# Other pairs, other shares: a change to the order and the engines of a Strassen weight gradient

## The chip, the cores and the metric

The kernel runs on one core of a Trainium2 chip. The metric is the device time of one execution in microseconds; the time before is 169.47 us, the median of three runs from 169.40 to 169.53. An instruction stands in one of five in-order queues: TensorE (PE, products), VectorE (DVE), ScalarE (ACT), GpSimd (POOL, which issues the loads here) and SyncE (SP, which issues the output).

## The reference

```python
def setup_inputs():
    batch, m, k, n = 16, 512, 1024, 768
    ...

def reference(input, grad_output):
    return np.einsum('bmk,bmn->kn', input, grad_output).astype(np.float32)
```

All 16 x 512 = 8192 rows are summed over: the output is X^T G, 1024 x 768, for X of 8192 x 1024 and G of 8192 x 768.

## The kernel before

**Slices and units.** The 8192 rows are 64 slices of 128 rows. Two slices make a unit; `LOADS` (line 11) has one letter for each of 32 units. An "s" unit is two plain items, one slice each. A "P" unit is one item, a Strassen pair. GpSimd loads every slice with two DMAs that turn float32 into bfloat16: G at line 100, X at line 102. Only slice 0 and slice 1's X come another way, as float32 over the queues of SyncE and ScalarE (lines 74 to 77), and are rounded by VectorE and ScalarE (`round_by`, line 191). The buffers of the loads are rings of 14 units (`PAIRS_HELD`); those of the sums of pairs are rings of 9 (`SUMS_HELD`). TensorE, VectorE and ScalarE keep the order in which the code records their instructions; for GpSimd's loads the order is made when the program is built.

**Quarters and products.** The output is cut into quarters A, B, C, D (A and B the upper 512 rows of k, A and C the left 384 columns). Each quarter takes four PSUM banks, one for each block q of 128 rows. A plain item gives A, B, C and D a product for each q: 16 matmuls of 128 x 128 by 128 x 384. A pair needs 28 matmuls instead of 32: 7 products m, n, o, p, q, A, D, four blocks each. For them VectorE makes six sums a pair (`sum_g1` to `sum_x3`, lines 114 to 143: g1 and g2 write `ge`, x1 and x2 write `xe`, g3 and x3 overwrite half of `gp` and `xp`). The products A and D go straight into the quarters; m to q are gathered in `macc` and added to the quarters at the end, in 24 "shares" (`top1` to `low3`, lines 154 to 174).

**Visits.** `ORDER` (line 14) writes the order of the work out by hand. "A6" means: bring stream A up to its item 6. A step with "!" closes the visit: its four banks are evicted into `acc` or `macc` (`shut`, line 275). Between opening and closing a visit holds half of PSUM (one of two `slots`), so two visits are open at once. The numbers are fills: the one ahead of the letter, and the four behind the "!", ahead of the eviction of each bank, say how many sums or shares VectorE does there; they are taken from one list, `filler` (line 176), sums first, pair by pair, then shares block by block (line 181).

**Evictions.** A bank is evicted either by VectorE, which adds it to the sum in SBUF (line 284; a copy, line 282, when the sum is new), or by ScalarE[...]: it copies the old sum into the bank before the visit (the "seed", line 256) and the bank back afterwards (line 280). `CARRIED` gives ScalarE blocks 2 and 3 of every visit but the last ones of the quarters.

**Start and end.** After ten wide and two narrow warm-up matmuls, the first products are A and C of slice 0; the right half of slice 0's G is rounded when step 2 is reached (line 335), on VectorE behind the evictions of C1. At the end the finished quarters leave in pieces of 192 KB (line 288); the last block of D is computed as 256 and 128 columns, so that its first part leaves sooner (lines 312 to 325).

Of the kernel before, what the change touches and what calls it, by code (L numbers as in the profile page):

```python
# [7 lines left out]

P = 128

LOADS = "sssPssssPsPsPPPPPPPPPPPPPPPsssss"


ORDER = (
    "A1 C1!0,0,0,0 D1 D2!0,0,0,0 A2 B1 B2 B3!0,0,0,0 A3 C4!0,0,0,0 A4 A5 B4 B5 B6!0,0,0,0 A6 "
    "C6!0,0,0,0 D6 6A7 D8!0,0,0,0 A8 o1!0,0,0,0 A9 B8!0,0,0,0 A10 C9 C10!0,0,0,0 A11 "
    "q1!0,0,0,0 A12 D12 A13 D13 A14!0,0,0,0 D14!0,0,0,0 n1 C14!0,0,0,0 B13 B14 6n2!0,0,0,0 "
    "B15 p1 p2!0,0,0,0 B16!0,0,0,0 m1 m2 A17!0,0,1,1 D18 4m3!0,0,0,0 D19 D20 B18!0,0,0,0 "
    "C18!0,0,1,1 A21 D21 4A22!0,0,0,0 D22 o4!2,0,1,1 q4 2D23!3,0,0,0 q5 n5 3n6!0,0,0,0 q6 p5 "
    "p6!6,0,0,0 q7 o7!1,0,0,2 m7 3q8!1,0,0,0 m8 A25 A26!5,0,0,0 m9 p9!1,0,0,2 D27 "  # L20
    "3m10!1,0,0,0 D28 n10!3,0,0,2 D29 A29!2,0,1,1 o11 2o12!2,0,0,0 D30 q12 4D31!1,0,0,0 q13 "
    "p12 p13!5,0,0,0 q14 m14!2,1,0,1 n14!2,0,0,2 q15 o15 4q16!0,0,0,0 o16 D34!2,0,1,1 "
    "A34!1,1,0,3 o17 n17 3o18!0,0,0,0 n18!0,0,0,0 A35 m18!0,0,0,0 A39 q18!0,0,0,0 p18!0,0,0,0 "
    "A41 A43 C22 C24 C26 A46!13,0,0,0 B23 B24 B28!6,0,0,0 C28!5,0,0,0 D46!0,0,0,0 "
).split()

WARMUP = [512] * 10 + [128] * 2
PAIRS_HELD = 14
SUMS_HELD = 9

CARRIED = (2, 3)
COPIED = CARRIED or (1, 3)


@with_exitstack
def kernel(
# [6 lines left out]
    nc = tc.nc  # L43
# [4 lines left out]
    _, _, N = grad_output.shape  # L48
    S = B * M // P
    KH = K // 2  # L50
    NH = N // 2
    Q = KH // P

    X = input.rearrange("b m k -> (b m) k")
    G = grad_output.rearrange("b m n -> (b m) n")
# [17 lines left out]
    gf = pairs.tile([P, N], f32, name="gf", tag="gp")  # L73
# [18 lines left out]
    xg = []  # L92
    for u, kind in enumerate(LOADS):
        pool = pairs if u else head
        xp = pool.tile([P, 2, K], bf16, name="xp", tag="xp")
        gp = pool.tile([P, 2, N], bf16, name="gp", tag="gp")
        for h in range(2):
            s = 2 * u + h
            if s > 0:
                nc.gpsimd.dma_start(out=gp[:, h, :], in_=G[s * P : (s + 1) * P, :])  # L100
            if s > 1:
                nc.gpsimd.dma_start(out=xp[:, h, :], in_=X[s * P : (s + 1) * P, :])  # L102
            if kind == "s":
                items.append(("s", xp[:, h, :], gp[:, h, :]))
        if kind == "P":
            items.append(("P", xp, gp))
        xg.append((xp, gp))
# [68 lines left out]
    filler = []  # L176
    for i, item in enumerate(items):
        if item[0] == "P":
            filler += [(f, i) for f in (sum_g1, sum_g2, sum_g3, sum_x1, sum_x2, sum_x3)]
    if filler:  # L180
        filler += [(f, q) for q in range(Q) for f in (top1, top2, top3)]
        filler += [(f, q) for q in range(Q) for f in (low1, low2, low3)]
    filler.reverse()

    def fill(n):
        for _ in range(n):
            f, i = filler.pop()
            f(i)


    def round_by(engine, dst, src, c0, c1):
        copy = nc.vector.tensor_copy if engine == "DVE" else nc.scalar.copy
        copy(out=dst[:, c0:c1], in_=src[:, c0:c1])  # L193

    x0, x1, g0 = items[0][1], items[1][1], items[0][2]
# [34 lines left out]
    def sum_of(p, q):  # L230
        if p in SLOT:
            return macc[:, SLOT[p], q, :]
        row = q if p in "AB" else Q + q
        return acc[:, row, 0:NH] if p in "AC" else acc[:, row, NH:N]

    done = {p: 0 for p in streams}
    fresh = {p: True for p in streams}
    slots = [0, 1]
    used = set()

    def visit(p, upto, close, ahead, last):
        items_now = streams[p][done[p] : upto]
        done[p] = upto
        opening = p not in opened
        if opening:

            tail = p in "ABCD" and streams[p][upto - len(items_now)] > LAST_PAIR - 2
            slot = slots.pop(0)
            banks = []
            for q in range(Q):  # L250
                name = f"bank{slot * Q + q}"
                bank = psum.tile([P, 512], f32, name=name)[:, 0:NH]
                carried = q in CARRIED and not fresh[p] and not tail
                if carried:
                    assert name in used
                    nc.scalar.copy(out=bank, in_=sum_of(p, q))  # L256
                used.add(name)
                banks.append((bank, carried))
            opened[p] = (slot, banks)
        slot, banks = opened[p]  # L260
        final = upto == len(streams[p])

        def mm(q, j):
            stat, mov = operands(p, items_now[j], q)
            bank, carried = banks[q]
            nc.tensor.matmul(  # L266
                bank,
                stat,
                mov,
                start=opening and j == 0 and not carried,  # L270
                stop=close and j == len(items_now) - 1,
                skip_group_check=carried,
            )

        def shut(q):
            fill(ahead[q])
            bank, carried = banks[q]
            dst = sum_of(p, q)
            if carried or (fresh[p] and q in COPIED):
                nc.scalar.copy(out=dst, in_=bank)  # L280
            elif fresh[p]:
                nc.vector.tensor_copy(out=dst, in_=bank)  # L282
            else:
                nc.vector.tensor_add(out=dst, in0=bank, in1=dst)  # L284
            if final and p in "ABCD":
                row = q if p in "AB" else Q + q
                c0 = 0 if p in "AC" else NH
                nc.sync.dma_start(out=OUT[:, row, c0 : c0 + NH], in_=dst)

        if len(items_now) == 1:  # L290
            for q in range(Q):
                mm(q, 0)
            if close:
                for q in range(Q):
                    shut(q)
        else:
            for q in range(Q):
                if last and q == Q - 1 and opening:
                    break
                for j in range(len(items_now)):  # L300
                    mm(q, j)
                if close:
                    shut(q)
            else:
                q = None
            if q is not None:

                fill(ahead[q])
                dst = sum_of(p, q)
                row = q if p in "AB" else Q + q  # L310
                b0 = 0 if p in "AC" else NH
                for c0, c1, name in ((0, 256, None), (256, NH, f"bank{slots[0] * Q}")):
                    bank = banks[q][0] if name is None else psum.tile([P, 512], f32, name=name)
                    for j in range(len(items_now)):
                        stat, mov = operands(p, items_now[j], q)
                        nc.tensor.matmul(  # L316
                            bank[:, 0 : c1 - c0],
                            stat,
                            mov[:, c0:c1],
                            start=j == 0,  # L320
                            stop=j == len(items_now) - 1,
                        )
                    d = dst[:, c0:c1]
                    nc.vector.tensor_add(out=d, in0=bank[:, 0 : c1 - c0], in1=d)  # L324
                    nc.sync.dma_start(out=OUT[:, row, b0 + c0 : b0 + c1], in_=d)
        if close:
            fresh[p] = False
            del opened[p]
            slots.append(slot)

    for n, step in enumerate(ORDER):
        step, _, ahead = step.partition("!")
        at = next(c for c in step if c.isalpha())
        before, upto = step.split(at)
        if n == 2:
            round_by("DVE", g0, gf, NH, N)
            round_by("DVE", x1, xf[1], 4 * P, 6 * P)
            round_by("ACT", x1, xf[1], 6 * P, 8 * P)
            round_by("DVE", x1, xf[1], 0, 2 * P)
            round_by("ACT", x1, xf[1], 2 * P, 4 * P)  # L340
        fill(int(before or 0))
        ahead = [int(a) for a in ahead.split(",")] if ahead else None
        visit(at, int(upto), ahead is not None, ahead, n == len(ORDER) - 1)
    assert not filler and not opened


# [28 lines left out]
```

## Time and profile before

| what | value |
|---|---|
| median of 3 runs | 169.47 us |
| the profiled execution, its span | 169.8 us, 168.0 us |
| matmuls: whole ones of 384 columns, parts of the last block, warm-up | 940, 24, 12 |
| ScalarE: evictions, seeds | 92 of 483 ns, 74 of 495 ns |
| VectorE: evictions that add, that copy | 89 of 553 ns, 18 of 553 ns |
| VectorE: long shares, short shares | 16 of 954 ns, 8 of 558 ns |
| sums of a pair: g1, g2, g3, x1, x2, x3 | 553, 353, 553, 687, 421, 688 ns |
| loads by GpSimd | 125, 8.5 us from issue to landing |
| output pieces | 17, about 2.0 us from issue to landing |

A row of the timeline gives start and length in us, the engine, the line, the operation and its tiles, how many followed each other, and in brackets how long the engine had been idle and what ended it. The slices are fortieths of the span, 4.2 us each; a digit is a tenth of busy time. [...]the starts in the timeline tell what one instruction keeps the engine from the next.

### The profile page before, as it was taken

The page shows a single profiled execution, that of the slowest core. Times are in us where ns is not written, and L with a number is a line of the kernel's source. Part 1 is how long each engine was busy: PE and PEld are TensorE (multiplying, and loading weights), DVE is VectorE, ACT ScalarE, POOL GpSimd, SP SyncE. Part 2 cuts the span into 40 slices and gives each one's busy share as a digit, 9 for nine tenths or more (in the row PEclk, how much of TensorE's full clock was granted, in tenths as well). Part 3 has the DMA queues.
Part 4 walks back from the last instruction along what each step waited for, and adds up shares of the span by engine and source line. Part 5 has one row for each costly group of instructions (what it writes and reads, how often), then busy time and mean ns, then how long its engine had stood idle before and what let it go on. Part 6 is the DMA issues. An engine that isn't in the chain of part 4 may idle for free.

```text
span 168.0 us, 2737 instructions
## 1 busy us (share of the span) xinstructions
PE 161.3 (96%) x976; PEld 95.3 (57%) x976; DVE 124.1 (74%) x248; ACT 73.3 (44%) x172; POOL 66.6 (40%) x129
## 2 busy tenths in 40 slices
PE   8799989999999999999999899999999999989991
PEld 2365545656666566555566466655666666556561
DVE  0642755307667686999999988999996179999992
ACT  3536608435456473654554643365655451000000
POOL 7444444454355444455444554445526430000000
PEclk9999999999999999999999999999999999999999
DMA  5999999999999999999999999999999999331546
GB/s 180 287 209 209 206 210 209 208 206 211 209 208 209 208 209 208 209 207 208 209 208 209 207 207 209 211 207 208 208 208 210 208 208 208 65 134 53 187 151 223
DMA packets 21036, 33.39 MB, mean 199 GB/s; under 512 B 2336, under 2 KB 12832, under 8 KB 21024
## 3 DMA queue, kind: packets, MB, share of 16 engines
q0 software_dynamic: 18000, 28.65, 93.2%
q1 hardware_dynamic: 2736, 3.54, 6.0%
q10 hardware_dynamic: 288, 1.05, 1.6%
q8 instruction: 7, 0.11, 0.3%
q14 instruction: 5, 0.04, 0.1%
HBM read 58.72 MB, written 3.15 MB: 368 GB/s over the span
## 4 chain that ended last, share of the span: by engine, by line
PE 74%; DMA 12%; DVE 9%; POOL 2%; issue 1%; DVEq 0%; POOLq 0%
PE bank L266 73%; DMA xp<-in_input_dram 12%; DVE acc L152 5%; DVE acc L163 1%; POOL gp L100 1%; DVE macc L284 1%; PE bank L316 1%; POOL xp L102 1%; DVE xp L143 0%; DVE xe L134 0%; DVE acc L284 0%; DVE gp L129 0%; DVE acc L324 0%; DVE ge L124 0%; DVE xe L138 0%
## 5 line engine op out<-in xcount | busy, mean ns | idle before, releaser
L266 PE MATMUL bank<-gp,xp 128*128 128x384 bf16 x582 | 102.2, 327 | 1.9 <-DVE gp L193 0.9
L266 PEld LDWEIGHTS <-xp 128*128 128x128 bf16 x724 | 70.6, 98 | 51.1 <-issue 2.7
L102 POOL DMA_DIRECT2D xp<-in_input_dram x62 | 33.0, 532 | 42.9 <-DMA xp<-in_input_dram 30.4
L100 POOL DMA_DIRECT2D gp<-in_grad_output_dram x63 | 33.7, 536 | 27.5 <-DMA gp<-in_grad_output_dram 16.0
L284 DVE TENSOR_TENSOR acc<-bank,acc 128x384 f32<-128x384 f32 x53 | 27.0, 553 | 15.2 <-PE bank L266 15.0
L280 ACT COPY acc<-bank 128x384 f32<-128x384 f32 x46 | 20.5, 483 | 31.6 <-PE bank L266 31.6
L280 ACT COPY macc<-bank 128x384 f32<-128x384 f32 x46 | 20.5, 483 | 31.0 <-PE bank L266 31.0
L266 PE MATMUL bank<-ge,xp 128*128 128x384 bf16 x142 | 28.7, 326 | 0.7 <-DVE xp L143 0.6
L266 PEld LDWEIGHTS <-xe 128*128 128x128 bf16 x216 | 21.1, 98 | 14.3 <-issue 0.4
L266 PE MATMUL bank<-gp,xe 128*128 128x384 bf16 x144 | 26.3, 326 | 0.0
L284 DVE TENSOR_TENSOR macc<-bank,macc 128x384 f32<-128x384 f32 x36 | 18.6, 554 | 7.7 <-PE bank L266 7.6
L256 ACT COPY bank<-acc 128x384 f32<-128x384 f32 x38 | 17.2, 495 | 0.0
L256 ACT COPY bank<-macc 128x384 f32<-128x384 f32 x36 | 16.3, 496 | 0.0
L152 DVE TENSOR_TENSOR acc<-acc,macc 128x768 f32<-128x768 f32 x16 | 15.3, 954 | 0.3
L266 PE MATMUL bank<-ge,xe 128*128 128x384 bf16 x72 | 13.0, 326 | 0.0
L143 DVE TENSOR_TENSOR xp<-xp 128x1024 bf16<-128x1024 bf16 x18 | 12.4, 688 | 0.0
L134 DVE TENSOR_TENSOR xe<-xp 128x1024 bf16<-128x1024 bf16 x18 | 12.4, 687 | 0.0
L120 DVE TENSOR_TENSOR ge<-gp 128x768 bf16<-128x768 bf16 x18 | 10.0, 553 | 1.0 <-DMA gp<-in_grad_output_dram 0.8
L129 DVE TENSOR_TENSOR gp<-gp 128x768 bf16<-128x768 bf16 x18 | 9.9, 553 | 0.0
L282 DVE COPY acc<-bank 128x384 f32<-128x384 f32 x8 | 4.1, 553 | 7.7 <-PE bank L266 7.7
L282 DVE COPY macc<-bank 128x384 f32<-128x384 f32 x10 | 5.1, 553 | 3.8 <-PE bank L266 3.8
L138 DVE TENSOR_TENSOR xe<-xp 128x512 bf16<-128x512 bf16 x18 | 7.6, 421 | 0.0
(18 smaller groups left out, 27.5 us busy)
## 6 DMA issues: line engine op xcount, KB each, us to landing
xp<-in_input_dram POOLq DMA_DIRECT2D x62, 256.0 KB, 8.5
gp<-in_grad_output_dram POOLq DMA_DIRECT2D x63, 192.0 KB, 8.5
out_dram<-acc SPq DMA_DIRECT2D x15, 192.0 KB, 2.0
xf<-in_input_dram ACTq DMA_DIRECT2D x2, 512.0 KB, 5.0
gf<-in_grad_output_dram SPq DMA_DIRECT2D x2, 192.0 KB, 4.5
out_dram<-acc SPq DMA_DIRECT2D x1, 128.0 KB, 2.1
out_dram<-acc SPq DMA_DIRECT2D x1, 64.0 KB, 1.8
```

What stands on the lines that cost most here:

```text
L100: nc.gpsimd.dma_start(out=gp[:, h, :], in_=G[s * P : (s + 1) * P, :])
L102: nc.gpsimd.dma_start(out=xp[:, h, :], in_=X[s * P : (s + 1) * P, :])
L120: nc.vector.tensor_add(out=ge[:, 0:2, :], in0=g[:, :, 0, :], in1=g[:, :, 1, :])
L129: nc.vector.tensor_sub(out=g[:, 1:3, :], in0=g[:, 1:3, :], in1=g[:, 3::-3, :])
L134: nc.vector.tensor_add(out=xe[:, 0:2, :].rearrange("p a k -> p (a k)"), in0=xp[:, 0, :], in1=xp[:, 1, :])
L143: nc.vector.tensor_sub(out=x[:, 1:3, :], in0=x[:, 1:3, :], in1=x[:, 0::3, :])
L152: nc.vector.tensor_add(out=dst, in0=dst, in1=macc[:, slots, q, :])
L256: nc.scalar.copy(out=bank, in_=sum_of(p, q))
L266: nc.tensor.matmul(bank, stat, mov, start=opening and j == 0 and not carried, stop=close and j == len(items_now) - 1, skip_group_check=car ...
L280: nc.scalar.copy(out=dst, in_=bank)
L282: nc.vector.tensor_copy(out=dst, in_=bank)
L284: nc.vector.tensor_add(out=dst, in0=bank, in1=dst)
```

## The change

`LOADS` has twenty pairs instead of eighteen: first eight plain units, then twenty pairs, then four plain units. `ORDER` is another list, and a step says how many banks of its visit ScalarE takes ("q4:4", "C16:3", "B24" with none): the last ones, with a seed where the sum is not new. The 24 shares get a list of their own, `SHARES`: first the four `top3`, then `low1` of three blocks, then the others, each kind over the blocks. The right half of slice 0's G is rounded at step 1, after A's visit of slice 0, whose banks are now evicted at once ("A1:2!0,0,0,0"), and before C's. `MERGED`, a way to load two slices with one DMA, is set to 99 and never applies. In the building, GpSimd's loads get another order in some places: slices 46 to 49 are issued as X46 X47 X48 X49 G46 G47 G48 G49, where before it was G46 X46 G47 X47 X48 X49 G48 G49.

```diff
-LOADS = "sssPssssPsPsPPPPPPPPPPPPPPPsssss"
+LOADS = "ssssssssPPPPPPPPPPPPPPPPPPPPssss"
...
 ORDER = (
-    "A1 C1!0,0,0,0 D1 D2!0,0,0,0 A2 B1 B2 B3!0,0,0,0 A3 C4!0,0,0,0 A4 A5 B4 B5 B6!0,0,0,0 A6 "
...
-    "A41 A43 C22 C24 C26 A46!13,0,0,0 B23 B24 B28!6,0,0,0 C28!5,0,0,0 D46!0,0,0,0 "
+    "A1:2!0,0,0,0 C1:2 D1:2 C2!0,0,0,0 D2 B1:4 B3!0,0,0,0 D3 A4:2 D4 A5!0,0,0,0 D5 C5:2 "
+    "C6!0,0,0,0 D6 D7 B5:2 D8!0,0,0,0 B8 A9:4!0,0,0,0 B9 B10 C10:4!0,0,0,0 B11 B12 D12:4!0,0,0,0 "
+    "B13 A14:2 A15 B14 B15 B16!0,0,0,0 A16 C16:3!0,1,3,2 A17!0,0,0,0 n1:2!0,0,0,0 D17:2 "
...
+    "3D27!3,0,0,0 o12 p12:2!1,0,0,2 m12:2!1,0,0,2 o13 1n13:3!2,0,1,2 o14 A29:2!3,0,0,0 q14:2 "
+    "3o15!2,0,0,0 q15 m15:2!1,0,0,1 D31:2!2,1,0,1 q16 p16:3!2,0,2,1 q17 n17:3!2,0,1,2 "
+    "A33:2!1,0,1,1 q18 D34:2!1,0,0,2 o19:2!1,0,0,2 m19:2 4q20!2,0,0,0 m20!0,0,0,0 D35:0 "
+    "n20:2!2,0,0,1 p20:2!1,1,0,1 D39 o20:4!3,0,0,0 D40!0,0,0,0 B19:0 C17:0 C18 B21 B22 B23 "
+    "B24!6,0,0,0 C19 C20 C21 A44:4!2,3,2,2 C24!0,0,0,0 D44:0!0,0,0,0 "
...
+SHARES = (
+    "t30 t31 t32 t33 l10 l11 l12 t20 t21 t22 t23 t10 t11 t12 t13 l20 l21 l22 l23 l13 l30 l31 l32 "
+    "l33 "
...
-CARRIED = (2, 3)
-COPIED = CARRIED or (1, 3)
...
-    if filler:
-        filler += [(f, q) for q in range(Q) for f in (top1, top2, top3)]
-        filler += [(f, q) for q in range(Q) for f in (low1, low2, low3)]
+    share_by = {"t1": top1, "t2": top2, "t3": top3, "l1": low1, "l2": low2, "l3": low3}
+    filler += [(share_by[c[:2]], int(c[2:])) for c in SHARES]
...
-                carried = q in CARRIED and not fresh[p] and not tail
+                act = q >= Q - byact
+                carried = act and not fresh[p]
...
-            if carried or (fresh[p] and q in COPIED):
+            if act:
                 nc.scalar.copy(out=dst, in_=bank)
...
+        if n == 1:
+            round_by("DVE", g0, gf, NH, N)
         if n == 2:
-            round_by("DVE", g0, gf, NH, N)
             round_by("DVE", x1, xf[1], 4 * P, 6 * P)
```

## The prediction, made before the changed kernel ran

> **What bounds the kernel now.** I read the page from the top: busy shares, the slices, then the chain that ended last, which lies on TensorE for 74%, on loads for 12% and on VectorE for 9%.
>
> ```profile
> PE 161.3 (96%) x976; PEld 95.3 (57%) x976; DVE 124.1 (74%) x248; ACT 73.3 (44%) x172; POOL 66.6 (40%) x129
> ...
> DVE  0642755307667686999999988999996179999992
> ...
> DMA  5999999999999999999999999999999999331546
> ```
>
> TensorE is the bound, but two others follow it closely: the loads fill the DMA engines for 34 slices (about 143 us), and VectorE is near full from 64 us on. So I read TensorE's timeline for what is lost at its own pace.
>
> ```profile
> 5.21 1.91 PE L266 MATMUL bank<-gp,xp 128*128 128x384 bf16 x8
> 8.01 14.63 PE L266 MATMUL bank<-gp,xp 128*128 128x384 bf16 x88 [0.89 <-DVE gp L193]
> ...
> 24.18 0.34 PE L266 MATMUL bank<-gp,xp 128*128 128x384 bf16 x1 [0.43 <-DMA xp<-in_input_dram]
> ...
> 96.12 2.77 PE L266 MATMUL bank<-ge,xp 128*128 128x384 bf16 x16 [0.58 <-DVE xp L143]
> ...
> 118.88 5.36 PE L266 MATMUL bank<-ge,xp 128*128 128x384 bf16 x32
> 124.08 0.81 PE L266 MATMUL bank<-gp,xp 128*128 128x384 bf16 x4
> ...
> 148.86 7.96 PE L266 MATMUL bank<-gp,xp 128*128 128x384 bf16 x48 [0.56 <-DVE acc L284]
> ```
>
> Pace: 32 products between 118.88 and 124.08, so 0.1625 us each. Number the 940 whole products from 0; stretch minus count times pace is the loss. From 5.21 to product 28 (11.26, twenty after 8.01): 1.50. To product 101 (24.18): 12.92 - 73 x 0.1625 = 1.06. To product 536 (96.12): 71.94 - 435 x 0.1625 = 1.25, of which 0.75 is the named wait. To product 856 (148.86): 52.74 - 320 x 0.1625 = 0.74. Then none. Sum 4.55. With 940 x 0.1625 = 152.75, 2.15 for the split last bank (162.50 to 164.65) and 3.38 of tail, 5.21 + 152.75 + 4.55 + 2.15 + 3.38 = 168.04: the span.
>
> Next, GpSimd's issues (the landing of the load eight earlier releases each) and VectorE's rows:
>
> ```profile
> 10.87 0.53 POOL L100 DMA_DIRECT2D gp<-in_grad_output_dram  x1 [0.72 <-DMA xp<-in_input_dram]
> ...
> 114.65 0.53 POOL L102 DMA_DIRECT2D xp<-in_input_dram  x1 [0.39 <-DMA gp<-in_grad_output_dram]
> ```
>
> ```profile
> 98.43 0.55 DVE L129 TENSOR_TENSOR gp<-gp 128x768 bf16<-128x768 bf16 x1
> 98.89 0.68 DVE L134 TENSOR_TENSOR xe<-xp 128x1024 bf16<-128x1024 bf16 x1
> 99.50 0.42 DVE L138 TENSOR_TENSOR xe<-xp 128x512 bf16<-128x512 bf16 x1
> 99.83 0.68 DVE L143 TENSOR_TENSOR xp<-xp 128x1024 bf16<-128x1024 bf16 x1
> 100.43 0.55 DVE L120 TENSOR_TENSOR ge<-gp 128x768 bf16<-128x768 bf16 x1
> 100.90 0.35 DVE L124 TENSOR_TENSOR ge<-gp 128x384 bf16<-128x384 bf16 x1
> ```
>
> Slice 2's X landed at 10.87. On VectorE starts count, not durations, since neighbours overlap: 0.47, 0.27, 0.47, 0.61, 0.33, 0.61 for g1, g2, g3, x1, x2, x3, together 2.76 a pair (0.27 is 83.67 to 83.94). An eviction takes 0.47, a long share 0.88 behind an independent instruction and 0.99 behind one on the same row. A result is usable 0.08 after its successor could start.
>
> **What the Trainium skill says.** "TensorE: Matmul & The Clock Gate", section "Back-to-back issue gap", gives N/2.4 + 2.5 ns; for N = 384 that is 162.5 ns, what the trace has. "PSUM — Partial Sum Buffer", section "Engine vs sequencer instructions", says that the queues of VectorE and ScalarE are strictly first in, first out, so one late sum holds every eviction behind it; the trace agrees (at 96.12 TensorE waits for an x3 put behind evictions). "DMA: Bandwidth & Descriptors", section "Queues, rings and completion order", says that each DMA engine consumes a ring's descriptors in ring order. The trace agrees: slices 48 and 49 were issued X, X, G, G, and the issue at 114.65, which needs the last of these four, came 4.4 us after the four began to land.
>
> **The change, part by part.**
>
> 1. Twenty pairs for eighteen remove 8 products: -1.30.
>
> 2. The start. G's right half is rounded after two evictions of A instead of two of C, so D1 starts near 7.0 instead of 8.01. But the new order needs slice 2 at product 25 (before: 28), and that lands at 10.87 in both. Product 28 then starts at 10.87 + 3 x 0.1625 = 11.36: loss 1.60 for 1.50. The sooner rounding is worth nothing; its cover is this landing.
>
> 3. No pair until slice 16. The waits before 24.18 (x3 of an early pair, then slice 8's X) go: slice 8 is first needed at product 111, 11.36 + 83 x 0.1625 = 24.85, after its landing at 24.1. Gain 1.06.
>
> 4. First pair. Its six sums follow the eviction of C16's first bank. Product 221, the last into it, starts at 42.72; an eviction starts 0.41 after (94.56 to 94.97 on ScalarE in the trace); 43.13 + 0.47 + 2.76 + 0.08 = 46.44. A17, product 240, is due at 45.81. New loss 0.63.
>
> 5. VectorE and ScalarE. Evictions: VectorE 108 to 84, ScalarE 92 to 120; seeds 74 to 92. Sums: 12 more, 6.5 us at full durations, against 24 x 0.553 = 13.3 taken away: VectorE gets 6.8 lighter. ScalarE gets 28 x 0.483 + 18 x 0.495 = 22.4 heavier, 96 of 168 us. All of it lies beside TensorE except where a seed is late. Before, all small waits between products 101 and 536 made 0.50; I keep 0.50 from 240 to 648 for seeds and late sums. Bounds: 0, and 1.2 if four-bank visits show their extra seeds. At D29 the wait (0.75) goes.
>
> 6. The late G. The built order of GpSimd's issues changes: slices 46 to 49 come as X46 X47 X48 X49 G46 G47 G48 G49 (before: G46 X46 G47 X47 X48 X49 G48 G49). G49 had landed before by 114.5, when VectorE began on it without idling. A slice takes 2.21 (X at 28.34, 30.56, 32.74), by bytes 0.95 for G and 1.26 for X. The bytes up to G49 are the same, so G47 lands at 114.5 - 2 x 0.95 = 112.6; in the old order it would be 3.8 sooner. Pair 15 (slices 46, 47) is what VectorE stands before then: it reaches that g1 near 110.4, behind m15's evictions. From 112.6: g1, g2, g3 1.21, D31's first eviction 0.47, x1 0.61, 0.08: 114.97. q16, product 648, needs x1 and is due at 46.44 + 408 x 0.1625 + 0.50 = 113.24. New loss 1.73. Twenty products later q17 (due 118.22) needs the next pair's x1; VectorE from 114.89: eviction 0.47, x2 0.33, x3 0.61, g1 0.47, eviction 0.47, g2 0.27, g3 0.47, x1 0.61, 0.08: 118.67. Loss 0.45. Queued behind the waiting g1 are D31's and p16's evictions, and p16's seeds on ScalarE.
>
> Note that the wait is on a landing: what is lost before it, up to 1.7 us, changes nothing at the end.
>
> 7. The shares one by one. Before, 13 of them stood in front of A46's evictions and made the 0.74 at 148.86; this goes. Late next is A44, whose four seeds follow B24's evictions. VectorE from q20's first eviction (product 753 + 0.41): 13 evictions 6.11, four short shares 1.88, eleven long ones at 0.90, 9.90: 17.9; then 0.08 and a seed, 0.50: 18.5. TensorE from there to A44, product 872: 119 x 0.1625 - 0.41 = 18.9. Cost 0, with 0.4 of cover. VectorE has hardly a gap there.
>
> 8. The end. From 118.67: 272 products 44.20, small waits 0.20, four products split in two 0.85 (12 cost 0.20 over pace before), tail 3.38 as before, since again nine output pieces (C24's and D44's) leave at the end: 167.3 against 168.03.
>
> Sum: **-0.73**. The profiled execution took 169.8, its span 168.0, so 1.8 lie around it; the median shown is 169.47, 0.3 lower. I put the difference on the median: **168.7**.
>
> **Rivals.**
> - The G loads are not late (slices 46 and 47 land in time although issued later). For: eight loads are in flight. Against: point 114.65 above. Then 1.73 + 0.45 go: 166.6.
> - ScalarE's seeds come late. Ten visits now have three or four seeds where all had two: 16 more at 0.41, 6.6 us. For: 22 us more on ScalarE. Against: even so it is idle 40% of the time, and what is lost ahead of product 648 is absorbed. If a tenth shows behind it: 169.4.
> - The closing stretch on VectorE becomes the bound (slower). Place: q20 to A44. If neighbours don't overlap there, evictions cost 0.553 for 0.47 (13 x 0.083 = 1.1) and shares 0.09 more (15 x 0.09 = 1.35): 2.4, less the cover of 0.4: 2.0 on TensorE, 170.7. It decides from 1.5 us of extra VectorE time, 0.4 of cover and the 1.1 to slower than 169.8. For: VectorE has no gap there. Against: the overlap shows in every pair of rows.
>
> **Numbers.** Forecast 0.62 (its own range 168.2 to 169.3), late G absent 0.13, late seeds 0.14, VectorE bound 0.11. A measurement of this kernel tells about 0.2%, 0.34 us, from no change: faster below 169.13. Faster: 0.13 and 0.54 of the 0.62, 0.67; slower: 0.11 and 0.01 of the seeds, 0.12; same: the other 0.08 and 0.13, 0.21. The range goes from 166.6 to 169.7 and leaves the slower case out.
>
> **What would show it.** Products in the changed trace: no idle between 11.4 and 45; waits for x3 near 46.4 (0.6), for x1 near 115 (1.7) and 118.7 (0.45); VectorE idle from 110.4 to 112.6 until a G lands; none at A44. Wrong would be: TensorE running through 113 to 115, or waiting on a seed for over 0.3 us anywhere.

## The result, and the profile after

The changed kernel takes 169.5 us (median of 4 runs, 169.44 to 169.74), as the kernel before does in the same comparison (169.5, 169.40 to 169.64): ratio (this kernel over the kernel before) 1.0002, 95% interval 0.9985 to 1.0019. Twenty-one more runs (e2 below) gave 0.9987 (0.9981 to 0.9994), so it is about 0.2 us faster. The forecast was 0.73 us. Two executions of the experiments below ran at a lower granted clock (e9: 212.5 us at 0.756; e10: 172.8 us at 0.948) and are in no ratio or mean given here.

The head of the page after: the span, the busy times, and the slices of VectorE and of the DMA engines.

```profile
span 167.4 us, 2778 instructions
...
PE 159.1 (95%) x960; PEld 93.6 (56%) x960; DVE 116.8 (70%) x236; ACT 93.4 (56%) x218; POOL 66.3 (40%) x129
...
DVE  0712220002789786999689999759889999999872
...
DMA  5999999999999999999999999999999999505275
```

The span fell from 168.0 to 167.4, and 167.3 was forecast. VectorE's busy time fell by 7.3 us (6.8 was forecast), ScalarE's rose by 20.1 (22.4). The dip "75" in VectorE's slices lies at 105 to 113 us. TensorE's timeline after:

```profile
5.17 1.48 PE L278 MATMUL bank<-gp,xp 128*128 128x384 bf16 x8 [0.30 <-DVE xp L203]
6.89 2.92 PE L278 MATMUL bank<-gp,xp 128*128 128x384 bf16 x17 [0.24 <-DVE gp L203]
10.71 35.11 PE L278 MATMUL bank<-gp,xp 128*128 128x384 bf16 x215 [0.89 <-DMA xp<-in_input_dram]
...
46.36 0.82 PE L278 MATMUL bank<-ge,xp 128*128 128x384 bf16 x4 [0.54 <-DVE xp L154]
...
110.76 2.76 PE L278 MATMUL bank<-ge,xp 128*128 128x384 bf16 x16
...
114.98 0.82 PE L278 MATMUL bank<-gp,xe 128*128 128x384 bf16 x4 [1.46 <-DVE xe L145]
...
118.65 3.42 PE L278 MATMUL bank<-gp,xe 128*128 128x384 bf16 x20 [0.25 <-DVE xe L145]
...
162.94 0.82 PE L328 MATMUL bank<-gp,xp 128*128 128x256 bf16 x8
```

The starts to compare with the forecast are 46.36, 114.98, 118.65 and 162.94: the first three were put at 46.44, 114.97 and 118.67. Of the kernel before's two waits here, the one for the rounded G has shrunk from 0.89 us (at 8.01) to 0.24 (at 6.89), and the one at 24.18 is gone: one row holds 215 products without a gap. A wait of 0.89 at 10.71, for slice 2's X, is new. VectorE's rows around the dip:

```profile
109.50 1.05 DVE L296 TENSOR_TENSOR macc<-bank,macc 128x384 f32<-128x384 f32 x2
112.56 0.56 DVE L131 TENSOR_TENSOR ge<-gp 128x768 bf16<-128x768 bf16 x1 [2.02 <-DMA gp<-in_grad_output_dram]
113.03 0.35 DVE L135 TENSOR_TENSOR ge<-gp 128x384 bf16<-128x384 bf16 x1
113.30 0.55 DVE L140 TENSOR_TENSOR gp<-gp 128x768 bf16<-128x768 bf16 x1
113.77 0.55 DVE L296 TENSOR_TENSOR acc<-bank,acc 128x384 f32<-128x384 f32 x1
114.24 0.68 DVE L145 TENSOR_TENSOR xe<-xp 128x1024 bf16<-128x1024 bf16 x1
```

VectorE stands for 2.02 us in front of g1 of pair 15 (L131), until slice 47's G lands; the bank's eviction (L296) and x1 (L145) follow it in the queue, and x1 is what TensorE waits for until 114.98. The chain that ended last runs over the same transfer:

```profile
95.03 8.29 DMA xp<-in_input_dram
103.32 0.28 issue
103.60 8.86 DMA gp<-in_grad_output_dram
...
112.56 0.56 DVE ge L131
```

So what was seen inside the span came as forecast. What did not is the time around it, what a run takes beyond its span (below: the time outside). Over 13 runs of the kernel before (e1) 1.77 us lie outside the span, over 21 runs of the changed one (e2) 2.13 us. Mean spans are 167.98 and 167.43. So the span gives 0.55 us, and 0.36 of it is lost outside.

### The profile page after: what moved, and what is told of

Its sections match the earlier page's. It is cut to its first block, busy times and chain, and to the rows that moved or that the text cites. A ratio compares the mean times of both kernels' runs of the same rounds, so it can differ in the third digit from the quotient of the medians.

```text
span 167.4 us, 2778 instructions
## 1 busy us (share of the span) xinstructions
PE 159.1 (95%) x960; PEld 93.6 (56%) x960; DVE 116.8 (70%) x236; ACT 93.4 (56%) x218; POOL 66.3 (40%) x129
## 4 chain that ended last, share of the span: by engine, by line
PE 74%; DMA 15%; DVE 6%; issue 2%; POOL 1%; DVEq 0%; POOLq 0%
PE bank L278 74%; DMA xp<-in_input_dram 10%; DMA gp<-in_grad_output_dram 5%; DVE xe L145 1%; POOL gp L111 1%; DVE ge L131 1%; DVE gp L140 1%; DVE xp L154 1%; DVE acc L296 1%; DVE xe L149 0%; DVE ge L135 0%; DVE acc L336 0%; DVEq L384 0%; DVE macc L296 0%; DVEq L131 0%
## 5 line engine op out<-in xcount | busy, mean ns | idle before, releaser
L278 PEld LDWEIGHTS <-xp 128*128 128x128 bf16 x700 | 68.1, 98 | 48.8 <-DMA xp<-in_input_dram 1.3
L278 PE MATMUL bank<-gp,xp 128*128 128x384 bf16 x540 | 93.1, 326 | 1.6 <-DMA xp<-in_input_dram 0.9
L296 DVE TENSOR_TENSOR acc<-bank,acc 128x384 f32<-128x384 f32 x42 | 21.6, 553 | 34.2 <-PE bank L278 33.8
L292 ACT COPY macc<-bank 128x384 f32<-128x384 f32 x65 | 28.7, 485 | 25.1 <-PE bank L278 24.9
L292 ACT COPY acc<-bank 128x384 f32<-128x384 f32 x55 | 24.9, 485 | 29.6 <-PE bank L278 29.2
L278 PEld LDWEIGHTS <-xe 128*128 128x128 bf16 x240 | 23.3, 98 | 17.7 <-DVE xe L145 2.5
L278 PE MATMUL bank<-gp,xe 128*128 128x384 bf16 x160 | 28.5, 326 | 1.7 <-DVE xe L145 1.7
L268 ACT COPY bank<-acc 128x384 f32<-128x384 f32 x45 | 20.3, 497 | 6.7 <-DVE acc L296 6.7
L268 ACT COPY bank<-macc 128x384 f32<-128x384 f32 x47 | 21.0, 495 | 1.3 <-DVE acc L296 1.3
L296 DVE TENSOR_TENSOR macc<-bank,macc 128x384 f32<-128x384 f32 x33 | 17.3, 554 | 3.4 <-PE bank L278 3.1
L145 DVE TENSOR_TENSOR xe<-xp 128x1024 bf16<-128x1024 bf16 x20 | 13.7, 684 | 0.0
L154 DVE TENSOR_TENSOR xp<-xp 128x1024 bf16<-128x1024 bf16 x20 | 13.7, 683 | 0.0
L131 DVE TENSOR_TENSOR ge<-gp 128x768 bf16<-128x768 bf16 x20 | 11.0, 551 | 2.3 <-DMA gp<-in_grad_output_dram 2.3
L135 DVE TENSOR_TENSOR ge<-gp 128x384 bf16<-128x384 bf16 x20 | 7.0, 351 | 0.0
```

Source lines behind the costliest of these rows:

```text
L131: nc.vector.tensor_add(out=ge[:, 0:2, :], in0=g[:, :, 0, :], in1=g[:, :, 1, :])
L145: nc.vector.tensor_add(out=xe[:, 0:2, :].rearrange("p a k -> p (a k)"), in0=xp[:, 0, :], in1=xp[:, 1, :])
L154: nc.vector.tensor_sub(out=x[:, 1:3, :], in0=x[:, 1:3, :], in1=x[:, 0::3, :])
L278: nc.tensor.matmul(bank, stat, mov, start=opening and j == 0 and not carried, stop=close and j == len(items_now) - 1, skip_group_check=car ...
```

## The experiments

The theories to be told apart were these. For the time outside: it hangs on the length of one engine's program (whose, was open), or on the work itself. For the time inside: the order of the loads costs some 1.8 us, and ScalarE's share of the banks, chosen per visit, is what makes twenty pairs possible.

### Both kernels again (e1, e2)

> The kernel before, unchanged but for one empty line, to get spans of ordinary runs. Theory 1 (the change did shorten the span, and the time outside the span differs between the programs): runs of about 169.5 us have spans near 167.7, so 1.8 us lie outside in every run, against 2.1 us for the changed kernel. Theory 2 (the profiled execution of before was an exception, and the prediction started from it): runs of about 169.5 us have spans near 167.4 with 2.1 us outside, and the profile has less lost on TensorE than the 4.55 us counted. Time 169.5 either way, ratio 1.000.

> The changed kernel, unchanged but for one empty line. Both theories: time 169.5, span 167.4, 2.1 us outside. If it comes out at a span of 167.7 or a time below 169.1, the result itself was not settled by its four runs.

Measured: before 169.69 (13 runs, ratio 1.0003, 0.9995 to 1.0012); after 169.55 (21 runs, ratio 0.9987, 0.9981 to 0.9994). The time outside was 1.72 to 1.81 in every run of the first, 2.07 to 2.19 in every run of the second: a step, not a scatter.

### Loads in the written order (e3, e4, e8)

GpSimd is put among the engines whose order is the code's, so that each slice is issued G, then X.

```diff
-    ctx.enter_context(tc.manual_schedule(engines={E.PE, E.DVE, E.Activation}))
+    ctx.enter_context(tc.manual_schedule(engines={E.PE, E.DVE, E.Activation, E.Pool}))
```

> The changed kernel with GpSimd's loads kept in the order in which the code writes them (G, X, G, X for all slices); the other engines' instructions are the same. Theory late G: the waits at products 648 and 668 (1.5 and 0.3 us in the changed kernel's profile) go, and slice 2's X lands one G sooner at the start (0.9 us less waiting at product 25): span 167.4 - 2.7 = 164.7, time 166.8, ratio 0.984. Rival, that the loads are the bound anyway and a landing waits elsewhere: span over 166.5, time over 168.6.

> The kernel before with GpSimd's loads in the written order, nothing else. Theory late G: no wait of the kernel before hangs on the order of loads except a few tenths at slice 2, which the early pair's x3 and slice 8's landing at 24.1 take back: time 169.3 to 169.6, ratio 0.999 to 1.001. Rival, that the written order is better for any kernel: ratio below 0.995.

The changed kernel gained: 167.3 us (166.9 to 168.7, 6 runs), ratio 0.9874 (0.9845 to 0.9904); the span is 164.8 to 165.2 in four of the six, 166.2 and 166.5 in two. In the profiled one of these two TensorE waited 1.53 us for an X landing near 22.6 us, as the kernel before waited for slice 8's. The kernel before gained nothing from the same edit: 169.75, ratio 1.0001 (0.9993 to 1.0009). The order of the loads is therefore a cost of the changed kernel, not of both.

To separate the late G from the start, e8 keeps this edit, and gives slices 2 and 3 both G before both X:

```diff
+        if u == 1:
+            for h in range(2):
+                nc.gpsimd.dma_start(out=gp[:, h, :], in_=G[(2 + h) * P : (3 + h) * P, :])
+            for h in range(2):
+                nc.gpsimd.dma_start(out=xp[:, h, :], in_=X[(2 + h) * P : (3 + h) * P, :])
...
-            if s > 0 and u < MERGED:
+            if s > 0 and u != 1:
...
-            if s > 1 and u < MERGED:
+            if s > 1 and u != 1:
```

> As the run with all loads in written order, but the loads of slices 2 and 3 stay as they were (G2 G3 X2 X3), so slice 2's X lands at 10.7 again. It splits that run's gain. Theory: the waits at 648 and 668 go, the wait at product 25 (0.9 us) stays and isn't absorbed later, now that no landing gates product 648: span 165.6 to 165.9, time 167.8. Rival, the start is worth nothing in any case: same time as the run with all loads in written order, 167.0 to 167.3.

Measured: 167.71 us (167.62 to 167.82, 4 runs), ratio 0.9881 (0.9867 to 0.9894), mean span 165.60. VectorE and TensorE of e8 where the changed kernel stood:

```profile
109.56 1.04 DVE L301 TENSOR_TENSOR macc<-bank,macc 128x384 f32<-128x384 f32 x2
110.52 0.55 DVE L136 TENSOR_TENSOR ge<-gp 128x768 bf16<-128x768 bf16 x1
```

```profile
46.43 0.82 PE L283 MATMUL bank<-ge,xp 128*128 128x384 bf16 x4 [0.54 <-DVE xp L159]
...
110.82 2.76 PE L283 MATMUL bank<-ge,xp 128*128 128x384 bf16 x16
113.42 0.81 PE L283 MATMUL bank<-gp,xe 128*128 128x384 bf16 x4
...
116.87 3.42 PE L283 MATMUL bank<-gp,xe 128*128 128x384 bf16 x20
...
161.16 0.82 PE L333 MATMUL bank<-gp,xp 128*128 128x256 bf16 x8
```

g1 now starts 0.96 us after the first of two evictions, with no wait; q16 follows at 113.42 at once (110.82 + 16 x 0.1625), and the last bank starts at 161.16 in place of 162.94. Up to 46.4 us the two kernels agree within 0.1. The late G thus cost 1.8 us of span (167.43 - 165.60), and it was the order of issue. The edit also puts the loads of slices 52 to 57, 62 and 63 in the written order, but these add nothing: the lead of e8 is 1.78 us at q17 (118.65 - 116.87) and still 1.78 at the last bank.

### ScalarE's share held at two banks (e7), or partly (e12)

```diff
-    "4q2:4!2,0,0,0 o2:4 D18 3o3!1,1,0,1 D19!0,0,0,0 p3:4 A19:2 3p4!2,0,1,0 A20!0,0,0,0 m3:4 m4 "
+    "4q2:2!2,0,0,0 o2:2 D18 3o3!1,1,0,1 D19!0,0,0,0 p3:2 A19:2 3p4!2,0,1,0 A20!0,0,0,0 m3:2 m4 "
...
```

and so with every 3 and 4 of the order.

> The changed kernel with ScalarE's share held at two banks a visit at most; the banks taken off it are added by VectorE. Some 27 banks move, 11 of them between 41 and 64 us, where VectorE then has 11 x 0.47 = 5.2 us more in a stretch in which it is busy about 7 us of 8. Theory, the choice per visit is what lets VectorE make the sums of twenty pairs in time: the sums of pairs 1 and 2 come late, 3 to 4 us are lost before 70 us, of which the wait for the late G (1.5 us) takes back part; span 170 to 171.5, time 172 to 173.5. ScalarE's stream is short again (248 instructions), so theory 1a has 1.8 outside. Rival, VectorE has room enough: time 169.5 or less.

Measured: 173.0 us, ratio 1.0192 (1.0178 to 1.0206), mean span 171.22, 1.77 us outside. TensorE waits for x3 (L154) three times where the changed kernel did once:

```profile
47.20 0.82 PE L278 MATMUL bank<-ge,xp 128*128 128x384 bf16 x4 [0.97 <-DVE xp L154]
...
57.39 0.82 PE L278 MATMUL bank<-ge,xp 128*128 128x384 bf16 x4 [1.56 <-DVE xp L154]
...
63.34 0.82 PE L278 MATMUL bank<-ge,xp 128*128 128x384 bf16 x4 [1.23 <-DVE xp L154]
```

Evictions given back to VectorE stand in front of the sums. The shares per visit are worth 3.8 us to this order (171.22 - 167.43); whether another order would do with two banks was not tried.

e12 is e8 with four of its eleven four-bank visits (p3, q4, o20, A44) at two:

> The same kernel with four of its ten four-bank visits (p3, q4, o20, A44) back at two banks each, which takes 14 evictions and seeds or so off ScalarE and moves 8 evictions to VectorE. Waits of the matmuls should grow by about 1.5 us where VectorE is short of time (slices 6 and 40 to 44), so that the span is 166.5 to 167.5 us. Theory that the outside time follows the number of ScalarE's evictions: between 1.77 and 2.12, or 1.77. Rival, that it follows something common to all kernels with twenty pairs and four-bank visits: 2.12.

Measured: 169.38 us, ratio 0.9978 (0.9969 to 0.9986), span 167.56, which is 2.0 over e8 and so a little outside what was expected, with 1.79 us outside the span. It showed that the 0.35 us outside can go with few edits, but it changed ScalarE's evictions and VectorE's length together.

### The time outside the span (e5, e6, e9 to e11, e13 to e17)

The first guesses were the lengths of the programs of ScalarE (244 instructions before, 306 after, with waits and branches) and of all engines together. (The kept traces list two instructions fewer for each engine in every run, 306 on VectorE for 308 and so on; the differences are the same.) Each was given to the kernel before in 62 instructions on one column, at the end of the program:

```diff
+    spare = accp.tile([P, 64], f32, name="spare")
+    one = nc.const_aps.tensor(1.0, (P, 1), f32)
+    for i in range(62):
+        nc.scalar.copy(out=spare[:, i : i + 1], in_=one)
```

> The kernel before with 62 one-column copies added at the end of ScalarE's stream, where ScalarE is idle from 139 us on, so that it has as many instructions (306 with waits) as in the changed kernel (before: 244). The output is the same. Theory 1a (the 0.35 us more outside the span come with ScalarE's longer stream): span 167.9 as before, outside 2.13 instead of 1.78, time 170.05, ratio 1.002. Rival 1b (they come from something else in the changed program, such as what its TensorE and VectorE streams hold): outside stays 1.78, ratio 1.000.

e6 has `nc.gpsimd.memset` in their place, and the loads in the written order.

> The kernel before with its loads in the written order (which alone changed nothing) and 62 one-column memsets at the end of GpSimd's stream, where GpSimd is idle from 136 us on: 237 instructions for 175. Theory 1a in the narrow form, ScalarE alone: outside stays 1.78. If the outside time goes by the number of instructions of the whole program, it is 2.13 here too; ratio 1.002.

Measured: 169.69 and 169.77 us, ratios 0.9998 (0.9990 to 1.0007) and 0.9999 (0.9991 to 1.0008), 1.77 and 1.79 us outside. Neither ScalarE's length nor the total is the cause. Then e8 got such instructions at its end, 24 on VectorE, 16 on ScalarE, or 16 on GpSimd:

> The changed kernel with slices 46 to 49 loaded G and X by turns, which took 167.71 us with 2.12 us of it outside the span, and 24 one-column copies more at the end of VectorE's program, so that VectorE holds as many instructions as in the kernel whose shares of banks were held at two (336 and 338 with waits), which had 1.77 us outside its span. Theory that the step of 0.35 us hangs on the length of VectorE's program: 1.77 us outside the span, and 167.4 us in all, or up to 0.5 more if the copies lie on the end of the span. Rival, that it hangs on what ScalarE is given in the middle of the program and not on VectorE's length: 2.12 us outside the span.

> The same kernel with 16 one-column copies more at the end of ScalarE's program. Theory that the outside time steps with the length of ScalarE's program, up at some lengths and down at others: 1.77 us outside the span and 167.4 us in all. Rival, that no engine's length sets it: 2.12 us outside and 167.7 us.

> The same kernel with 16 one-column memsets more at the end of GpSimd's program. Theory that GpSimd's length, whose DMA issues feed the whole kernel, sets the step: 1.77 us outside the span and 167.4 us. Rival: 2.12 us outside and 167.7 us.

Measured: e9 ratio 0.9901 (0.9884 to 0.9917), mean span 166.20, 1.76 us outside; e10 0.9884 (0.9865 to 0.9904), span 165.60, 2.15 outside; e11 0.9893 (0.9878 to 0.9908), span 165.40, 2.44 outside. So VectorE's count took the step away (though its copies, at the end, made the span 0.6 longer), ScalarE's did nothing, and GpSimd's added 0.3. Set beside VectorE's counts, all kernels so far but e11 fall in place: 308 before, 320 in e12, 336 in e7 and 338 in e9 with 1.76 to 1.79 us outside; 314 in after, e3, e8 and e10 with 2.12 to 2.15. Of the next five runs four change only this count, at places where TensorE doesn't wait for VectorE, and e16 only GpSimd's:

```diff
+        if step == "n1":
+            spare = accp.tile([P, 64], f32, name="spare")
+            one = nc.const_aps.tensor(1.0, (P, 1), f32)
+            for i in range(6):
+                nc.vector.tensor_copy(out=spare[:, i : i + 1], in_=one)
```

(in the kernel before; in the changed ones at the step "B11").

> The kernel before with six one-column copies more on VectorE, at a place where it waits for 4.2 us, so that its program has 314 instructions, as many as in the changed kernel (308 without them). Theory that the time outside the span hangs on the length of VectorE's program: the span stays at 168.0 us, 2.13 us lie outside it in place of 1.77, and the run takes 170.05 us. Rival, that it hangs on other work that the change brings: 1.77 us outside, 169.7 us.

> The changed kernel with slices 46 to 49 loaded G and X by turns (167.7 us, 2.12 us of it outside a span of 165.6), and six one-column copies more on VectorE in a stretch in which it waits, so that its program has 320 instructions in place of 314. Theory of VectorE's length: 1.77 us outside the span, 167.35 us in all, the best of these kernels. Rival: 2.12 us outside, 167.7 us.

> The changed kernel itself, with the same six copies on VectorE (320 instructions in place of 314). Theory of VectorE's length: 1.77 us outside a span of 167.4 us, 169.2 us in all, so 0.3 to 0.4 us below the changed kernel. Rival: 2.13 us outside, 169.55 us.

> The kernel before with 17 one-column memsets more at the end of GpSimd's program, 192 instructions in all, as in the run in which 16 of them raised the time outside the span from 2.12 to 2.44 us; 62 of them (237 instructions) had cost the kernel before nothing. Theory that GpSimd's length has such a step too, at 192 and not at 176 or 237: 2.1 us outside the span and 170.05 us. Rival, that the 0.32 us there came of the changed kernel's own end: 1.77 us outside and 169.7 us.

> The kernel before with twelve one-column copies more on VectorE where six were, so that its program has 320 instructions. Theory that the count itself decides (high at 314, low at 308 and 320): 1.77 us outside the span, 169.75 us. Rival, that copies of this kind, or any length over 308 in this kernel, bring the 0.35 us: 2.1 us or more outside, 170.1 us or more.

| kernel | VectorE's count | us, median | ratio (interval) | mean span | outside |
|---|---|---|---|---|---|
| e1, before | 308 | 169.69 | 1.0003 (0.9995 to 1.0012) | 167.98 | 1.77 |
| e13, before and 6 | 314 | 170.12 | 1.0020 (1.0011 to 1.0030) | 168.00 | 2.11 |
| e17, before and 12 | 320 | 169.66 | 0.9996 (0.9987 to 1.0004) | 167.92 | 1.77 |
| e2, after | 314 | 169.55 | 0.9987 (0.9981 to 0.9994) | 167.43 | 2.13 |
| e15, after and 6 | 320 | 169.14 | 0.9962 (0.9947 to 0.9977) | 167.38 | 1.77 |
| e8, loads by turns | 314 | 167.71 | 0.9881 (0.9867 to 0.9894) | 165.60 | 2.12 |
| e14, e8 and 6 | 320 | 167.46 | 0.9861 (0.9845 to 0.9877) | 165.65 | 1.80 |

Six copies make the kernel before slower and the changed one faster, and twelve do nothing to the kernel before. The copies in e13's profile, on VectorE, between an eviction and the next:

```profile
39.14 1.01 DVE L285 TENSOR_TENSOR acc<-bank,acc 128x384 f32<-128x384 f32 x2
40.07 0.45 DVE L346 COPY spare<-const-float32-1.0 128x1 f32<-128x1 f32 x6
40.64 1.21 DVE L285 TENSOR_TENSOR acc<-bank,acc 128x384 f32<-128x384 f32 x2
```

They end at 40.5, before the bank's eviction is due, and the mean span is unchanged to 0.02 us. So at these counts it is the number of instructions on VectorE that decides, and the kind of work put in plays no part. e16, 17 memsets on GpSimd in the kernel before (192 instructions, as in e11), took 169.71 us with 1.77 outside: GpSimd's count alone has no such step there, and why e11 had 0.3 more stays open (its trace is read in the last section).

### Both together (e18)

> The changed kernel with all loads in the written order (167.3 us median, 166.9 to 168.7, with 2.14 us outside the span) and the six copies on VectorE (320 instructions). Theory of the count: 1.77 us outside, a median of about 167.0, 166.6 at the lowest and up to 1.7 more in executions where a landing near 22 us is late. Rival: as without the copies, 167.3.

Measured: 166.74 us (166.56 to 168.09, 4 runs), ratio 0.9841 (0.9802 to 0.9879), 1.78 outside; the 168.09 has a span of 166.3 against 164.8 to 165.0 in the others. Loads wholly in order and 320 instructions on VectorE make the fastest of these kernels, 3.0 us below the 169.75 of the kernel before beside it; e14, at 167.37 to 167.50, is the steadiest.

## Why the forecast went wrong, point by point

**The step that failed is the last one**: "The profiled execution took 169.8, its span 168.0, so 1.8 lie around it; the median shown is 169.47, 0.3 lower. I put the difference on the median". This carries the time around the span over to the changed kernel unchanged, and gives no reason for it. It was 1.77 before and 2.13 after: 0.36 us more, half of the forecast. That it is this term is shown by e15: the changed kernel with 320 instructions on VectorE in place of 314, and 1.77 us outside, takes 0.9962 of the kernel before (0.9947 to 0.9977), or 0.64 us less; the forecast of -0.73 was 0.9957.

Two smaller parts of the miss are no step of the argument. The steps below are counted on two profiled executions whose spans are 0.67 us apart (168.03 and 167.36), while the mean spans are 0.55 apart. And the level of 168.7 started from a median of three runs, 169.47, which lay 0.24 below that of 43 runs of the kernel before (169.71).

The steps inside the span held, with errors of up to 0.22 us each:

- Readings. The pace of 0.1625 held. The section that the prediction names for it calls the formula the gap of a product on its own, and gives less for a stream of weight loads and products; here it is such a stream, with a weight load for every product (x960 each), that keeps 0.1625. VectorE's slices are at 9 from 67 us on, not from 64; nothing rested on that.
- Steps 2 and 3 (start): slice 2's X landed a little sooner (10.71 for 10.87) and covered the sooner rounding, as forecast. D1 did start sooner, 6.89 for 8.01, and TensorE stood again until 10.71.
- Step 4 (first pair): 46.36 for 46.44, the wait named as x3's.
- Step 5 (small waits): 0.50 was kept up to q16. After 46.36, 408 products should end at 112.66; those that ran ended at 110.76 + 16 x 0.1625 = 113.36, where q16 was due. So the small waits were 0.70.
- Step 6 (late G): q16 at 114.98 lost 1.62 (1.73 forecast); q17 at 118.65, due 20 products later at 118.23, lost 0.42 (0.45). VectorE stood from 110.5 to 112.56, where 110.4 to 112.6 was forecast. Against e8, the whole is 1.8 and not the sum 2.04, since e8 loses 0.20 at q17 too: 113.42 + 20 x 0.1625 = 116.67, but it starts at 116.87. The first rival, G not late, fell.
- Step 7 (the 24 shares): no wait at A44. Of the rivals, neither late seeds (none of the named waits of TensorE, those over 0.15 us, is on ScalarE) nor a bound on VectorE showed.
- Step 8 (end): 272 products took 44.29, of which 0.09 is waiting (0.20 kept); the split bank took 0.82 to 163.76 (0.85); the tail took 3.60, and 3.38 was put. Before, SyncE began to issue the last two output pieces as TensorE ended, at 164.65; after, it began 0.39 us behind TensorE's end, at 164.15, directly after the piece ahead of them, whose issue ended at 164.06. Most likely the shorter bank (0.82 for 2.15) covers less of the adds and issues that come before these two, but no run tests it. What follows took 3.38 before and 3.21 after; why it is 0.17 shorter stays open. The rows, of after and then of before:

```profile
163.62 0.61 DVE L336 TENSOR_TENSOR acc<-bank,acc 128x256 f32<-128x256 f32 x2
164.15 0.90 SPq L337 DMA_DIRECT2D out_dram<-acc  x2
```

```profile
164.65 0.90 SPq L325 DMA_DIRECT2D out_dram<-acc  x2
```

Summed, -0.08 at the first pair, +0.20, -0.11, -0.03, -0.11, -0.03 and +0.22 make +0.06: the span is 167.36 for 167.3. The waits came where they were put; that the sum is so close is in part luck, since errors of +0.42 and -0.36 cancelled.

What the change is worth, by the runs: in this order the twenty pairs need ScalarE's shares per visit (3.8 us, e7); with them and loads by turns the span would fall by 2.4 us (e8); the order in which the build put the loads takes 1.8 of these back; and the count on VectorE takes 0.36 of the remaining 0.55.

## What to carry to other kernels

When products are removed, look at what feeds the next wait: here eight loads in another order took back three quarters of what the pairs had gained, and one line that fixes the order of the issues returned it. A forecast of half a per cent has to treat the time outside the span as a quantity of its own: read span and run time of both kernels side by side before explaining a difference by anything in the trace. A few tiny instructions, where an engine waits anyway, are a cheap test of it.

## What the runs showed that was not expected

- The time outside the span takes two values, 1.76 to 1.80 us (308, 320, 336 or 338 instructions on VectorE) and 2.11 to 2.15 us (314), in 17 of 18 series of runs; e11, with 2.44, is the exception. The difference lies behind the span. The kept traces record semaphore updates there, which the views of the profile don't list, and nine updates of one semaphore close each of the twenty records. From the fifth, 1.68 to 1.73 us after the span's end, to the sixth it is 0.10 us at all other counts and 0.45 to 0.46 at 314, e11 included. In nineteen of the twenty the time outside is then the place of the ninth update less 0.12 to 0.14 us, so nothing differs ahead of the span. In e11 0.36 us more lie behind the ninth. What is waited for there, what in VectorE's count sets it, and where the step lies between 308 and 320 was not settled.
- In the changed kernel with all loads in the written order (e3, e18), 3 of 10 runs have longer spans (166.2 to 166.5 against 164.8 to 165.2). In the one of them that was profiled TensorE waited 1.53 us for an X near 22 us; that the other two have the same cause is not shown. With both G of slices 2 and 3 ahead of both X (e8, e14) none of 8 runs is longer; the cause was not looked for.
- "DMA: Bandwidth & Descriptors", section "Queues, rings and completion order", of the Trainium skill, says that each DMA engine consumes a ring's descriptors in ring order; it says so of the queues of SyncE and ScalarE, and adds that completion need not keep the order of issue. The late G are GpSimd's loads, and for them the trace agrees with the order: slice 47's G, issued at 103.60 behind four X and slice 46's G, landed 8.86 us later, about as long as loads take here (8.5 us before). In e8 it was issued at 100.16, and VectorE did not wait for it. What made it late was its place.
